# Gate chunks evicted by a plain copy, their sigmoid moved to the merge of the branches

## The chip, the cores and the metric

The kernel runs on one core of a Trainium2 chip. The metric is the device time of one execution in microseconds (us). The engines of the core are TensorE (PE for its matmuls, PEld for its weight loads), VectorE (DVE), ScalarE (ACT), GpSimd (POOL) and SyncE (SP); here POOL and SP mostly issue transfers. A matmul writes to PSUM, and another engine has to evict the result before the bank can be written again. Each engine takes its instructions in a fixed order. That order is settled when the program is built, by a scheduler that places one instruction after another.

## What is computed

One block of a hybrid network on 512 tokens of width 1024: a projection `u = h @ w_in`, two branches on it (RWKV time mixing and latent attention), a gated merge of the branches, an output projection, and then a large expert layer. What matters here is how the gates enter:

```python
u = h @ w_in[i]
gates = jax.nn.sigmoid(u[..., RW_COLS + MLA_COLS:]).reshape(B, T, N_BRANCHES, D)
...
merged = gates[:, :, 0] * (y_rw @ w_br_rwkv[i]) + gates[:, :, 1] * (y_mla @ w_br_mla[i])
x = x + merged @ w_out[i]
```

## The kernel before

Activations lie transposed, features on the partitions and 512 tokens along the free axis. The 4384 columns of `w_in` are taken in 35 chunks of 128, each a weight tile of 512 KB. Every product is formed in three parts from a high and a low half (`mm3`, L137): `hi*xh`, `hi*xl`, `lo*xh`. The high half of a weight is made by ACT (`whi`, L132), the low half by DVE (`wlo`, L133); L147 and L148 do the same for activations (`split`). A chunk with its 8 contraction steps is 24 matmuls.

The last 16 chunks are the gates, 8 for each branch. `gates` (L633) computes a chunk with `uchunk`, takes the sigmoid on ACT straight from PSUM into a tile `gt` (L637), and SP stores it to `gates_d` in DRAM (L638). Six gate chunks fill in beside the preparation of the time mixing (`prep`, PSUM tag `u` with one bank), four follow while DVE computes a triangular inverse (`inverse`, L555), and six stand before the recurrence (`chain`), beside the first steps of the attention (`attn`).

In `prep` ACT computes sigmoids (`sg` L416, `a` L420), exponentials (`E` L425) and square roots (L213), in the attention exponentials (`e` L879). Where the next function is not in the table that ACT holds, a table load stands in its order (ACT_TABLE_LOAD). A plain copy needs none in any of these places.

The merge comes after the branches. `wbr(1)` (L962) multiplies the attention's output with `w_br` in 8 units of 12 matmuls, one for each chunk of 128 outputs, and `wbr(0)` does the same for the time mixing. For every unit a gate chunk is fetched from `gates_d` by POOL's queue (L970) into a tile `gt` that has two buffers. In the first half the product `gt * ps` goes to `mp` (L980). In the second half `gt * ps` (L1002) and the sum with `mp` (L1003) are written in place, and `split` makes the halves `mh` and `ml` (L1004), so a buffer is free again only after `ml`. The 16 fetches are called the 1st to the 16th gate below, in the order of use. The PSUM tag `mm` has two banks, so a unit can start only when the product two units before it is done. Between the units ACT and DVE also convert weights: those of `w_br`, the input `pT` (`ph`, `pl`) and the two weights `w_pp`, whose raw tile is single-buffered. Then `w_out` follows in 8 chunks of 24 matmuls (L1006), which contract over all `mh` and `ml` and use the same two banks, and then the expert layer, by far the longest part.

Of the kernel before, what the change touches and what calls it, by code (L numbers as in the profile page):

```python
# [25 lines left out]
AF = mybir.ActivationFunctionType  # L26
# [86 lines left out]
def phase1(nc, tc, A, dbg):  # L113
# [10 lines left out]
    def wload(src, pl=None, row=False):  # L124
        own = pl is s.E or pl is s.PL
        raw = (pl if own else s.W).tile([128, 8, 128], F32, name="wraw", bufs={s.E: RAWB, s.PL: 1}[pl] if own else 3)
        nc.sync.dma_start(raw, src)
        s.nw += 1
        pl = pl or (s.WX if s.WX and s.nw % 3 == 0 else s.W)
        hi = pl.tile([128, 8, 128], F32R, name="whi", **(dict(tag="row", bufs=ROWS) if row else {}))  # L130
        lo = pl.tile([128, 8, 128], F32R, name="wlo", **(dict(tag="row", bufs=ROWS) if row else {}))
        nc.scalar.activation(hi, raw, AF.Copy)  # L132
        (nc.gpsimd if s.nw <= NWP else nc.vector).tensor_sub(lo, raw, hi.bitcast(F32))  # L133
        return hi, lo
    s.wload = wload

    def mm3(out, hi, lo, xh, xl, ks):  # L137

        n = len(ks)
        for i, (kw, kx) in enumerate(ks):  # L140
            nc.tensor.matmul(out, hi[:, kw], xh[:, kx], start=(i == 0), stop=False)  # L141
            nc.tensor.matmul(out, hi[:, kw], xl[:, kx], start=False, stop=False)  # L142
            nc.tensor.matmul(out, lo[:, kw], xh[:, kx], start=False, stop=(i == n - 1))  # L143
# [37 lines left out]
    def mm_tile(shape=(128, 512), tag="mm"):  # L181
        return (ppc if tag in "cu" else pp).tile(list(shape), F32, name=tag, tag=tag, bufs=1 if tag == "u" else None)
# [76 lines left out]
    def uchunk(oc, tag="mm", pl=None, raw=None):  # L259
        hi, lo = raw or wload(A["w_in"][oc], pl)  # L260
        ps = mm_tile(tag=tag)
        mm3(ps, hi, lo, *(XR if raw else (xh, xl)), [(k, k) for k in range(8)])
        return ps
# [369 lines left out]
    def gates(i0, i1, tag="u", pl=None):  # L633
        for i in range(i0, i1):
            ps = uchunk(19 + i, tag, pl)
            gt = MU.tile([128, T], F32, name="gt")
            nc.scalar.activation(gt, ps, AF.Sigmoid)  # L637
            nc.sync.dma_start(gates_d[i], gt)  # L638
            yield UNS

    oth = itertools.chain(others(), gates(0, NG))
    drive(prep(), oth)
    for _ in oth:
# [174 lines left out]
    def attn():  # L818
# [68 lines left out]
        def trans(n):  # L887
            e = EU[n]
            pt = mm_tile((128, 4, 128), tag="c" if n >= TC else "mm")
            for kb in range(4):  # L890
# [56 lines left out]
    for _ in gates(NG, NG + GK, GT):  # L947
        pass
# [3 lines left out]
    for _ in gates(NG + GK, 16, GT, GW):  # L952
        pass
# [8 lines left out]
    def wbr(b):  # L962
        for j in range(4):
            hi, lo = wload(A["w_br"][b * 4 + j])
            for o in range(2):
                oc = j * 2 + o
                ps = mm_tile(tag="mm")
                mm3(ps, hi, lo, yh, yl, [(o * 4 + k, k) for k in range(4)])
                gt = HM.tile([128, T], F32, name="gt")
                nc.gpsimd.dma_start(gt, gates_d[b * 8 + oc])  # L970
                yield oc, ps, gt

    HM = pool(name="hm", bufs=2, side="right")
# [5 lines left out]
    for oc, ps, gt in wbr(1):  # L979
        nc.vector.tensor_mul(mp[:, oc], gt, ps)  # L980
# [13 lines left out]
    for oc, ps, gt in wbr(0):  # L994
        if oc == 0:
            praw = PL.tile([128, 8, 128], F32, name="wraw", bufs=1)
            nc.sync.dma_start(praw, A["pT"].rearrange("p a (b t) -> p (a b) t", t=128))
            plh = PL.tile([128, 8, 128], F32R, name="ph", bufs=1)
            pll = PL.tile([128, 8, 128], F32R, name="pl", bufs=1)
            split(plh, pll, praw)  # L1000
            pw = [wload(A["w_pp"][k].rearrange("p (k c) -> p k c", k=8), PL) for k in range(2)]
        nc.vector.tensor_mul(gt, gt, ps)  # L1002
        nc.vector.tensor_add(gt, gt, mp[:, oc])  # L1003
        split(mh[:, oc], ml[:, oc], gt)  # L1004
    s.nsum = mm_tile((128, 4, 1), "s")
    for oc in range(8):  # L1006
        hi, lo = wload(A["w_out"][oc])
        ps = mm_tile()
# [8 lines left out]
    for tb in range(4):  # L1017
        for half in range(2):
            ps = mm_tile()
# [24 lines left out]
GT = "mm"  # L1044
EN = "a"
NWP = 0
TC = 99
LT_ = 2
LP = 3
# [498 lines left out]
```

## Time and profile before

| | us |
|---|---|
| median of three runs (1907.16 to 1909.44) | 1909.21 |
| the profiled execution, its own time | 1906.74 |
| its span, first to last instruction | 1904.8 |
| around the span (1906.74 - 1904.8) | 1.9 |
| PE busy | 1817.9 (95%) |
| DVE busy | 1540.0 (81%) |
| ACT busy | 830.6 (44%) |

The kernel falls into stretches: preparation with the first gates (to about 250 us), inverse with the other gates (250 to 323), recurrence and attention (to 484), merge (484 to 539), output projection and norm (to about 600), expert layer (to the end). A share of busy time is an average over all of them; what a change in one stretch is worth is read from the instructions there and from what each was waiting for.

### The profile page before, as it was taken

How to read it: one execution, taken by the hardware profiler on the slowest of the kernel's cores; microseconds unless marked ns; L12 is line 12 of the kernel's file. 1: busy time of each engine (PE TensorE's matmuls, PEld its weight loads, DVE VectorE, ACT ScalarE, POOL GpSimd, SP SyncE). 2: the span in 40 equal slices, each digit the busy share in tenths (PEclk: the TensorE clock that was granted, in tenths of full speed). 3: DMA queues.
4: the chain of work that ended last, by engine and by line, in shares of the span. 5: the costliest groups of instructions: out<-in, count | busy, mean ns of one | idle time of the engine just before them, and what ended most of it. 6: DMA issues, size and time to landing. Idle time of an engine off the chain costs nothing.

```text
span 1904.8 us, 29766 instructions
## 1 busy us (share of the span) xinstructions
PE 1817.9 (95%) x10969; PEld 1568.0 (82%) x10969; DVE 1540.0 (81%) x3103; ACT 830.6 (44%) x1227; POOL 464.4 (24%) x449
## 2 busy tenths in 40 slices
PE   8999868998999998999999999999999999999997
PEld 6777646776777888999999988888888888888775
DVE  7766778898855889999998956878787888777777
ACT  5656434665323334344444543333333333333354
POOL 1111321220101000332332021334344444344000
PEclk9999979998999999999999999999999999999999
DMA  4355655762434333789999799899999999999862
GB/s 170 117 154 150 184 161 167 224 200 83 149 105 143 101 101 94 240 307 360 359 340 345 281 348 350 312 346 343 326 335 333 344 351 347 327 334 338 291 215 99
DMA packets 196721, 470.19 MB, mean 247 GB/s; under 512 B 33312, under 2 KB 100896, under 8 KB 192736
## 3 DMA queue, kind: packets, MB, share of 16 engines
q1 hardware_dynamic: 146688, 273.23, 43.3%
q0 software_dynamic: 49744, 194.80, 29.1%
q8 instruction: 86, 1.41, 0.3%
q14 instruction: 59, 0.48, 0.1%
q10 hardware_dynamic: 144, 0.26, 0.0%
HBM read 397.97 MB, written 70.25 MB: 246 GB/s over the span
## 4 chain that ended last, share of the span: by engine, by line
PE 71%; DVE 12%; issue 7%; DMA 5%; ACT 3%; POOL 1%; SPq 0%; POOLq 0%; DVEq 0%; ACTq 0%
PE po L1498 26%; PE pa L1150 6%; PE pa L1148 6%; PE pa L1149 6%; PE mm L141 3%; PE mm L142 3%; PE mm L143 3%; PE po L1377 2%; DVE wlo L133 2%; PE q L141 2%; PE q L142 2%; PE q L143 2%; PE c L464 1%; DMA gt<-gates_d 1%; PE g L1178 1%
## 5 line engine op out<-in xcount | busy, mean ns | idle before, releaser
L132 ACT ACTIVATE whi<-wraw 128x1024 fp32r<-128x1024 f32 x352 | 370.6, 1059 | 457.5 <-PE pa L1149 156.0
L133 DVE TENSOR_TENSOR wlo<-wraw,whi 128x1024 fp32r<-128x1024 f32 x352 | 427.7, 1220 | 96.8 <-ACT whi L132 89.7
L1150 PE MATMUL pa<-hh,wlo 128*128 128x384 f32 x1024 | 347.8, 340 | 4.9 <-DVE wlo L133 4.8
L1148 PE MATMUL pa<-hh,whi 128*128 128x384 f32 x1024 | 348.8, 341 | 2.3 <-ACT ga L1156 1.3
L1149 PE MATMUL pa<-hl,whi 128*128 128x384 f32 x1024 | 347.5, 339 | 0.0
L1085 POOL DMA_INDIRECT row<-in_u,e x128 | 163.3, 1276 | 421.4 <-DVE row L1093 328.6
L1498 PE MATMUL po<-wlo,wh 128*128 128x512 f32 x768 | 237.2, 390 | 0.3 <-DVE wlo L133 0.3
L1085 POOL DMA_INDIRECT row<-in_v,e x128 | 176.4, 1378 | 249.4 <-DVE acc L1103 216.7
L1498 PE MATMUL po<-whi,wl 128*128 128x512 f32 x768 | 237.1, 389 | 0.0
L1498 PE MATMUL po<-whi,wh 128*128 128x512 f32 x768 | 210.4, 390 | 7.4 <-ACT whi L132 4.9
L1103 DVE SCALAR_TENSOR_TENSOR acc<-row,pre,acc 128x1024 f32<-128x1024 f32 x127 | 162.8, 1282 | 62.8 <-DMA row<-in_v,e 62.3
L1150 PEld LDWEIGHTS pa<-hh,wlo 128*128 128x128 f32 x1024 | 193.1, 189 | 7.8 <-DVE wlo L133 5.9
L1148 PEld LDWEIGHTS pa<-hh,whi 128*128 128x128 f32 x1024 | 193.2, 189 | 6.5 <-ACT ga L1156 1.7
L1149 PEld LDWEIGHTS pa<-hl,whi 128*128 128x128 f32 x1024 | 193.2, 189 | 3.6
L1498 PEld LDWEIGHTS po<-whi,wh 128*128 128x128 f32 x768 | 143.0, 188 | 33.6 <-ACT whi L132 6.2
L1498 PEld LDWEIGHTS po<-whi,wl 128*128 128x128 f32 x768 | 144.2, 188 | 30.5
L1093 DVE SCALAR_TENSOR_TENSOR row<-row,h2t 128x1024 f32<-128x1024 f32 x128 | 155.3, 1217 | 13.8 <-DMA row<-in_u,e 13.5
L1498 PEld LDWEIGHTS po<-wlo,wh 128*128 128x128 f32 x768 | 143.4, 188 | 27.5 <-DVE wlo L133 0.7
L147 ACT ACTIVATE wh<-gl 128x384 fp32r<-128x384 f32 x72 | 37.8, 526 | 204.9 <-PE po L1498 204.9
L141 PE MATMUL mm<-xh,whi 128*128 128x512 f32 x184 | 74.6, 406 | 4.4 <-ACT gt L637 3.3
L147 ACT ACTIVATE wh<-ga 128x384 fp32r<-128x384 f32 x48 | 25.1, 524 | 116.5 <-PE po L1498 74.2
L142 PE MATMUL mm<-xl,whi 128*128 128x512 f32 x184 | 74.1, 403 | 0.0
(465 smaller groups left out, 3160.6 us busy)
## 6 DMA issues: line engine op xcount, KB each, us to landing
wraw<-in_uT SPq DMA_DIRECT2D x128, 512.0 KB
wraw<-in_v SPq DMA_DIRECT2D x128, 512.0 KB
gd<-st POOLq DMA_DIRECT2D x12, 2048.0 KB, 10.3
g<-gd SPq DMA_DIRECT2D x32, 768.0 KB
wraw<-in_w_in SPq DMA_DIRECT2D x35, 512.0 KB
pk<-pk_d SPq DMA_DIRECT2D x16, 1024.0 KB
ga_d<-gs SPq DMA_DIRECT2D x72, 192.0 KB
gl<-ga_d SPq DMA_DIRECT2D x72, 192.0 KB
```

What stands on the lines that cost most here:

```text
L132: nc.scalar.activation(hi, raw, AF.Copy)
L133: (nc.gpsimd if s.nw <= NWP else nc.vector).tensor_sub(lo, raw, hi.bitcast(F32))
L141: nc.tensor.matmul(out, hi[:, kw], xh[:, kx], start=(i == 0), stop=False)
L142: nc.tensor.matmul(out, hi[:, kw], xl[:, kx], start=False, stop=False)
L143: nc.tensor.matmul(out, lo[:, kw], xh[:, kx], start=False, stop=(i == n - 1))
L1085: nc.gpsimd.indirect_dma_start(out=r, out_offset=None, in_=table, in_offset=bass.IndirectOffsetOnAxis(ap=e3[:, hk:hk + 1], axis=0))
L1093: nc.vector.scalar_tensor_tensor(r, r, 1.0, h2t, op0=OP.mult, op1=OP.mult, accum_out=pre[:, u:u + 1])
L1103: nc.vector.scalar_tensor_tensor(acc, r, pre[:, u:u + 1], acc, op0=OP.mult, op1=OP.add)
L1148: nc.tensor.matmul(pa, hi[:, k], hh[:, k, 0:NDT], start=(k == 0), stop=False)
L1149: nc.tensor.matmul(pa, hi[:, k], hl[:, k, 0:NDT], start=False, stop=False)
L1150: nc.tensor.matmul(pa, lo[:, k], hh[:, k, 0:NDT], start=False, stop=(k == 7))
L1498: nc.tensor.matmul(po[tb][:, half], w[:, ts], v[:, hs], start=(m == 0 and w is wh and v is vh), stop=(m == 127 and w is wl))
```

## The change

The sigmoid in `gates` becomes a plain copy, put in a block of higher priority for the scheduler, with an offset of 1000 places. `gates_d` then holds values before the sigmoid. In `wbr` the sigmoid is taken in place on the fetched tile. Everything else is as it was.

```diff
@@ -634,7 +634,9 @@
         for i in range(i0, i1):
             ps = uchunk(19 + i, tag, pl)
             gt = MU.tile([128, T], F32, name="gt")
-            nc.scalar.activation(gt, ps, AF.Sigmoid)
+
+            with tc.high_priority(offset=EP):
+                nc.scalar.activation(gt, ps, AF.Copy)
             nc.sync.dma_start(gates_d[i], gt)
             yield UNS
 
@@ -968,6 +970,7 @@
                 mm3(ps, hi, lo, yh, yl, [(o * 4 + k, k) for k in range(4)])
                 gt = HM.tile([128, T], F32, name="gt")
                 nc.gpsimd.dma_start(gt, gates_d[b * 8 + oc])
+                nc.scalar.activation(gt, gt, AF.Sigmoid)
                 yield oc, ps, gt
 
     HM = pool(name="hm", bufs=2, side="right")
@@ -1044,6 +1047,7 @@
 GT = "mm"
 EN = "a"
 NWP = 0
+EP = 1000
 TC = 99
```

Line numbers of the changed kernel are two to four higher behind the first edit: its copy is L639, its fetch L972, its sigmoid L973, the products L983 and L1005, the sum L1006.

How the order of instructions moves is shown at three places, from the two built programs.

**ACT, beside the preparation**, at the first gate chunk (`whi` is a weight's high half, `sg` and `a` are the preparation's sigmoids, `E` its exponential). Before:

```order
L132 ACTIVATE whi<-wraw 128x1024
L637 ACT_TABLE_LOAD
L637 ACTIVATE gt<-u 128x512
L416 ACTIVATE sg<-c,vec 128x512
L420 ACTIVATE a<-c,vec 128x512
L440 ACTIVATE a<-a,oka,vec 128x512
L132 ACTIVATE whi<-wraw 128x1024
L425 ACT_TABLE_LOAD
```

Now:

```order
L132 ACTIVATE whi<-wraw 128x1024
L639 ACTIVATE gt<-u 128x512
L416 ACT_TABLE_LOAD
L416 ACTIVATE sg<-c,vec 128x512
L420 ACTIVATE a<-c,vec 128x512
L440 ACTIVATE a<-a,oka,vec 128x512
L132 ACTIVATE whi<-wraw 128x1024
L425 ACT_TABLE_LOAD
```

The copy stands where the sigmoid stood, and the load goes to the next sigmoid of the preparation. Over all 16 chunks the eviction keeps its place among its neighbours; the table loads at L637 (six) and at L879 (two) are gone, and four new ones stand at L416. Up to the merge PE, DVE, POOL and SP keep their order.

**ACT and DVE, in the merge**, from the conversion of `pT` on. ACT before (`mh` is the high half of the merged product):

```order
L147 ACTIVATE ph<-wraw 128x1024
L132 ACTIVATE whi<-wraw 128x1024 x4
L147 ACTIVATE mh<-gt 128x512
L132 ACTIVATE whi<-wraw 128x1024
L147 ACTIVATE mh<-gt 128x512
```

ACT now (the four sigmoids before these rows are those of the 1st to 4th gate; the first of them has a table load):

```order
L147 ACTIVATE ph<-wraw 128x1024
L973 ACTIVATE gt<-gt 128x512 x2
L132 ACTIVATE whi<-wraw 128x1024 x2
L973 ACTIVATE gt<-gt 128x512 x2
L132 ACTIVATE whi<-wraw 128x1024 x2
L973 ACTIVATE gt<-gt 128x512 x2
L132 ACTIVATE whi<-wraw 128x1024
L147 ACTIVATE mh<-gt 128x512 x2
L132 ACTIVATE whi<-wraw 128x1024
L973 ACTIVATE gt<-gt 128x512 x2
L147 ACTIVATE mh<-gt 128x512 x2
```

DVE before, from the first product of the second half on:

```order
L1002 TENSOR_TENSOR gt<-gt,mm 128x512
L1003 TENSOR_TENSOR gt<-gt,mp 128x512
L133 TENSOR_TENSOR wlo<-wraw,whi 128x1024
L148 TENSOR_TENSOR ml<-gt,mh 128x512
L1002 TENSOR_TENSOR gt<-gt,mm 128x512
L133 TENSOR_TENSOR wlo<-wraw,whi 128x1024
L1003 TENSOR_TENSOR gt<-gt,mp 128x512
L1002 TENSOR_TENSOR gt<-gt,mm 128x512
L148 TENSOR_TENSOR ml<-gt,mh 128x512
```

DVE now:

```order
L133 TENSOR_TENSOR wlo<-wraw,whi 128x1024 x2
L1005 TENSOR_TENSOR gt<-gt,mm 128x512
L1006 TENSOR_TENSOR gt<-gt,mp 128x512
L1005 TENSOR_TENSOR gt<-gt,mm 128x512
L133 TENSOR_TENSOR wlo<-wraw,whi 128x1024
L1006 TENSOR_TENSOR gt<-gt,mp 128x512
L148 TENSOR_TENSOR ml<-gt,mh 128x512 x2
L133 TENSOR_TENSOR wlo<-wraw,whi 128x1024
L1005 TENSOR_TENSOR gt<-gt,mm 128x512 x2
L1006 TENSOR_TENSOR gt<-gt,mp 128x512 x2
L148 TENSOR_TENSOR ml<-gt,mh 128x512 x2
```

The gates are now handled in pairs: both sigmoids, both products, both sums, both high and both low halves. The sigmoids of the 9th and 10th gate stand behind the second `whi` of the pair before them, which is that of the second `w_pp` weight.

**PE, behind the merge**, in the first two chunks of `w_out` (numbers tell the two PSUM tiles apart: `mm_5274` and `mm_5308` before, `mm_5290` and `mm_5324` now). Before, the last rows of both:

```order
L141 MATMUL mm_5308<-mh_5071,whi_5304 128x512
L141 MATMUL mm_5274<-mh_5071,whi_5270 128x512
L142 MATMUL mm_5308<-ml_5072,whi_5304 128x512
L143 MATMUL mm_5308<-mh_5071,wlo_5305 128x512
L141 MATMUL mm_5308<-mh_5071,whi_5304 128x512
L142 MATMUL mm_5274<-ml_5072,whi_5270 128x512
L143 MATMUL mm_5274<-mh_5071,wlo_5271 128x512
L142 MATMUL mm_5308<-ml_5072,whi_5304 128x512
L143 MATMUL mm_5308<-mh_5071,wlo_5305 128x512
```

Now, around the last rows of the first:

```order
L142 MATMUL mm_5290<-ml_5080,whi_5286 128x512
L143 MATMUL mm_5290<-mh_5079,wlo_5287 128x512
L141 MATMUL mm_5290<-mh_5079,whi_5286 128x512
L142 MATMUL mm_5290<-ml_5080,whi_5286 128x512
L143 MATMUL mm_5290<-mh_5079,wlo_5287 128x512
L143 MATMUL mm_5324<-mh_5079,wlo_5321 128x512
L141 MATMUL mm_5324<-mh_5079,whi_5320 128x512
L142 MATMUL mm_5324<-ml_5080,whi_5320 128x512
```

Before, the first chunk ends two matmuls ahead of the second; now it ends 19 matmuls ahead of it (its 24th matmul is the 29th of the 48).

## Rows read from the trace of the kernel before

**Rows 1.** the page: busy time, share of the span, instructions by engine

```profile
PE 1817.9 (95%) x10969; PEld 1568.0 (82%) x10969; DVE 1540.0 (81%) x3103; ACT 830.6 (44%) x1227; POOL 464.4 (24%) x449
```

**Rows 2.** stretches: busy us of each engine, then TensorE's granted clock, DMA share, GB/s

```profile
60.00:250.00 190.00, 179.99 (x924) 137.91 (x922) 132.61 (x208) 106.35 (x139) 49.45 (x68) 0.98 0.58 161
250.00:330.00 80.00, 62.45 (x235) 47.37 (x235) 64.92 (x167) 30.02 (x44) 11.95 (x17) 0.87 0.45 145
...
484.00:512.00 28.00, 27.38 (x118) 21.16 (x119) 22.69 (x47) 10.35 (x14) 4.31 (x9) 1.00 0.57 177
512.00:539.12 27.12, 23.18 (x89) 17.10 (x88) 18.56 (x26) 8.70 (x11) 3.76 (x7) 0.94 0.51 159
539.12:552.00 12.88, 12.16 (x51) 9.29 (x51) 6.28 (x9) 3.48 (x6) 0.00 (x0) 1.00 0.17 56
552.00:640.00 88.00, 84.57 (x392) 68.49 (x393) 56.12 (x183) 32.33 (x48) 8.77 (x12) 1.00 0.37 120
```

**Rows 3.** waits of PE, 60 to 250 us: total, times, longest; the longest one

```profile
PE c L488 <- DVE bk L480: 3.8, 1, 3.8
```

**Rows 4.** timeline of ACT, front part: start us, us, line, tiles, [idle before]

```profile
74.10 1.28 ACT L637 ACT_TABLE_LOAD   x1
75.40 0.60 ACT L637 ACTIVATE gt<-u 128x512 f32<-128x512 f32 x1
79.18 0.69 ACT L416 ACTIVATE sg<-c,vec 128x512 f32<-128x512 f32 x1 [3.19 <-PE c L414]
...
250.86 1.28 ACT L637 ACT_TABLE_LOAD   x1
...
325.66 1.28 ACT L879 ACT_TABLE_LOAD   x1
```

**Rows 5.** timeline of PE, then DVE, front part

```profile
252.80 0.79 PE L141 MATMUL mm<-xh,whi 128*128 128x512 f32 x1 [3.32 <-ACT gt L637]
272.74 0.80 PE L831 MATMUL mm<-wlo,cqh 128*128 128x512 f32 x1 [5.79 <-DVE wlo L133]
...
257.05 0.91 DVE L567 TENSOR_TENSOR xtmp<-U,X 128x31 f32<-128x31 f32 x2 [6.83 <-DMA U<-pk_d]
...
330.02 0.21 DVE L880 RECIPROCAL mx<-mx 128x1 f32<-128x1 f32 x2
```

**Rows 6.** timeline of ACT in the merge

```profile
515.42 1.06 ACT L132 ACTIVATE whi<-wraw 128x1024 fp32r<-128x1024 f32 x1 [3.99 <-DMA wraw<-in_w_pp]
```

**Rows 7.** timeline of POOL in the merge; then all gate DMAs' time to landing

```profile
518.64 0.54 POOL L970 DMA_DIRECT2D gt<-gates_d  x1 [5.47 <-DVE ml L148]
523.02 0.54 POOL L970 DMA_DIRECT2D gt<-gates_d  x1 [3.83 <-DVE ml L148]
537.55 0.54 POOL L970 DMA_DIRECT2D gt<-gates_d  x1 [2.17 <-DMA wraw<-in_w_out]
...
DMA to landing us min/median/max: 2.7/3.0/4.8
```

**Rows 8.** timeline of DVE in the merge

```profile
513.39 0.68 DVE L1002 TENSOR_TENSOR gt<-gt,mm 128x512 f32<-128x512 f32 x1
538.29 0.69 DVE L1002 TENSOR_TENSOR gt<-gt,mm 128x512 f32<-128x512 f32 x1 [1.03 <-PE mm L143]
```

**Rows 9.** timeline of PE in the merge and after it

```profile
527.17 0.50 PE L141 MATMUL mm<-yh,whi 128*128 128x512 f32 x1 [1.87 <-DVE gt L1002]
539.12 0.47 PE L141 MATMUL mm<-mh,whi 128*128 128x512 f32 x1 [0.86 <-DVE gt L1002]
550.96 0.50 PE L141 MATMUL mm<-mh,whi 128*128 128x512 f32 x1 [0.50 <-ACT whi L132]
551.90 0.50 PE L141 MATMUL mm<-mh,whi 128*128 128x512 f32 x1 [0.22 <-ACT whi L132]
```

**Rows 10.** groups by line, ACT: busy us, mean ns, idle before

```profile
L1027 ACT ACTIVATE pst<-mm 128x512 f32<-128x512 f32 x8 | 4.8, 600 | 8.7 <-DMA pp_d<-pst 7.7 <-PE mm L1025 0.7 <-PE pa L227 0.3
L538 ACT ACTIVATE lg<-lg 128x512 f32<-128x512 f32 x1 | 0.6, 632 | 0.9 <-DVE lg L369 0.9
```

## The prediction, made before the result was known

> **What bounds the kernel now.** Read the page's busy times first: TensorE is busy 95% of the span, ACT 44% [rows 1]. Less work on ACT is therefore worth nothing by itself; only what TensorE waits for counts. The table of stretches says where TensorE has room: from 60 to 250 us it is busy 179.99 of 190 us at clock 0.98, from 250 to 330 only 62.45 of 80 at 0.87, in the first half of the merge 27.38 of 28, in its second half 23.18 of 27.12 at 0.94, and behind it in the expert layer 84.57 of 88 [rows 2]. Two consequences. A delay at the end of the merge is not made good later, as the expert layer has 3.4 us of slack in 88 and that slack sits in its own dependences: I carry a delay over one to one. And the change can matter in three places only: the front, where table loads go; the second half of the merge, where sigmoids come; and the start of `w_out`.
>
> Then the waits of TensorE in the first gates' stretch: the longest is 3.8 us, for DVE (`bk`, L480) [rows 3]; none of its long waits is for the gate eviction. The single one anywhere that is, stands at 252.80 [rows 5].
>
> **The front: copies for sigmoids.** The eviction itself keeps its price. The sigmoid out of PSUM takes 0.60 us [rows 4], a plain copy of the same shape out of PSUM 0.600 [rows 10]. It keeps its place too: in the built order copy and sigmoid have the same neighbours, so the "at once" of the edit, its priority block, moves nothing. What goes is table loads, 1.28 us each [rows 4]: six at L637 and two at L879 go, four come at L416, so ACT saves 4 x 1.28 = 5.1 us by these counts. Where do they lie?
>
> - In the preparation the load moves from ahead of the eviction to ahead of `sg`. There ACT had waited 3.19 us for TensorE's `c` [rows 4], so the new load lies in that wait. TensorE is nearly full in this stretch and waits for DVE: gain 0. ACT's 106.35 of 190 us [rows 2] says the same.
> - At 250.86 the load goes with nothing in its place. The eviction ends 1.28 us sooner, and TensorE, which had waited 3.32 us for it, starts at 251.5 instead of 252.80. What is late next? DVE's inverse starts at 257.05, after 6.83 us of waiting for a transfer (`U` from `pk_d`), and TensorE later stands 5.79 us at 272.74 for a `wlo` that DVE makes between inverse steps [rows 5]. The 1.28 us fill that wait. Gain 0, at best 1.3 if the `wlo` moves too.
> - The load at 325.66 [rows 4] stands ahead of an attention exponential; the pass behind it needs a DVE row that is made at 330.02 [rows 5]. Gain 0.
>
> So the front gives 0 (0 to -1.3).
>
> The Trainium skill, "ScalarE: Activation LUTs", section "Table sets: the hidden batching unit", says to batch activations by set; this change does so, and speaks for a gain. Its section "What ACT_TABLE_LOAD costs" adds a drain of about 1.38 us to a load of 1.283 us. By that page four loads would be an estimated 10.6 us of ACT's time. The trace agrees on the load (1.28) and shows no drain: the activation at 75.40 begins 0.02 us after the load's end [rows 4].
>
> **The merge's first half.** Eight sigmoids and one load are added. TensorE is full here (27.38 of 28) [rows 2], and a fetched gate waits for its product; a sigmoid of 0.63 us, the price of one from SBUF to SBUF [rows 10], fits between. Cost 0 (0 to 0.6).
>
> **The merge's second half** is where the added sigmoids reach the path. SP's and POOL's queues keep their order, but what POOL's fetches wait for becomes later. Step by step:
>
> 1. The sigmoids of the 9th and 10th gate stand, on ACT, behind the `whi` of the second `w_pp` weight, which waits 3.99 us for its transfer and runs 515.42 to 516.48 [rows 6]. So the 9th product, at 513.39 before [rows 8], starts at 516.48 + 0.6 = 517.05: 3.7 us later.
> 2. `mh` and `ml` of the 9th now stand behind the 10th's product and sum. From the 9th product to the fetch of the 11th: four passes of 0.69 [rows 8] and one weight conversion (1.06 on ACT [rows 6], not less on DVE) with the handovers, 4.1 to 5.2 us; before it was 518.64 - 513.39 = 5.25 [rows 7, 8]. I take 4.85: fetch of the 11th at 521.9, 3.3 late. The 12th follows one pass later, about 522.5, against 523.02: 0.5 us early. The even gates keep their times, the odd ones lose.
> 3. From then on a pair is a loop, since two buffers hold two gates: landing 3.0 [rows 7], sigmoid 0.63 [rows 10], products of both, sum, high and low half at 0.69 each [rows 8] = 3.4, together 7.1. With handovers, and a `w_out` conversion in one of them, 7.3 to 8.3; I take 7.9. The 15th gate is fetched at 521.9 + 2 x 7.9 = 537.7, and its product starts at 537.7 + 3.0 + 0.63 = 541.3, against 538.29 [rows 8]: +3.0.
> 4. `w_out` needs the bank that this product frees. Before it started 0.83 us after the product's start, at 539.12 [rows 8, 9]; now at 542.1. **+3.0** (+1.8 by 7.3, +3.8 by 8.3).
>
> **Behind it.** In `w_out` the first chunk's last matmul is now the 29th of 48 instead of the 46th. The conversions of the third weight are thus covered, where TensorE had waited 0.50 and 0.22 us [rows 9]: -0.7, up to -1.4 if the wait's second half goes too. I take **-1.0**.
>
> **The clock.** With the same TensorE work until then, TensorE stands about 3 us more in this half, mostly in one wait just ahead of `w_out`. Such waits have been followed by the lower clock here: the half with the wait of 1.87 us at 527.17 has a mean granted clock of 0.94, or (1 - 0.94) x 27.12 = 1.6 us lost; 250 to 330 has 0.87, 10.4 us lost over some four long waits, 2.6 each. After a wait of 0.86 us the clock stayed at 1.00 [rows 2, 9]. An added wait of 3 us lies nearer to the former: **+2.1** (0 to +2.6).
>
> **Sum:** 0 + 0 + 3.0 - 1.0 + 2.1 = +4.1 us. Against the profiled execution's own 1906.74 us that is 1910.8; the median of before is 2.5 us above it, and by the median the forecast is 1909.21 + 4.1 = **1913.3 us**. A measurement of this kernel tells about 0.2%, 3.8 us, from no change, so the forecast lies just above that line.
>
> **The rivals.**
>
> - *Faster: the front is paced by ACT.* If the loads lay on the path in spite of ACT's 44%, the net four would give 4 x 1.28 = 5.1 us: 1904.1 us. For it speaks TensorE's wait of 3.32 us at 252.80, which the load made longer [rows 5]; against it the 3.8 us wait for DVE and the 3.19 us of ACT waiting for TensorE [rows 3, 4]. It decides if the merge costs under 1.3 us. Chance 0.10. By the Trainium skill's batching rule and its 2.66 us for a switch ("ScalarE: Activation LUTs", "What ACT_TABLE_LOAD costs") the time would be an estimated 1898.6; the missing drain speaks against it.
> - *Within 0.2%: no clock loss.* The merge goes as above, but TensorE's added wait is cut into two or three short ones, since the even gates keep their schedule. Then the 2.1 us fall away: +2.0, 1911.2 us. For it speaks the clock of 1.00 after 0.86 us [rows 2, 9]. Chance 0.32.
> - *Slower still: paired fetches collide.* Two fetches now go out 0.6 us apart, each of 256 KB, together with weights. Landing is 3.0 us in the median and 4.8 at most [rows 7]. With 4.8 in the three pairs, +5.4: 1918.7 us. Against it: the fetches of before stood beside the same weight traffic and had 3.0. Chance 0.10.
> - *The change doesn't do what it says.* That the copy is not "at once" is settled by the built order, and is in the forecast; this has no chance of its own.
>
> **How the numbers follow.** Forecast 0.48, of which 0.08 falls below the 0.2% line as its terms vary; no clock loss 0.32; faster 0.10; colliding fetches 0.10. Faster by over 0.2% 0.10; within 0.32 + 0.08 = 0.40; slower 0.40 + 0.10 = 0.50. Range: the low end has -1.3 in the front, +1.8, -1.4 and no clock loss, -0.9, so 1908.3; the high end +3.8 - 0.7 + 2.6 and one landing of 4.8 instead of 3.0, +7.5, so 1916.7. Rounded outward, 1908 to 1917; the first and the third rival stay outside, 2 in 10.
>
> **What would show it.** In the timeline of ACT the loads ahead of gate evictions are gone, those at L416 end before the `c` they wait for, and the merge begins within 1.3 us of its old time; a start 3 us or more earlier proves the front wrong. In the merge, the 9th sigmoid starts right after a `whi`, the 11th gate is fetched near 521.9 and the 12th near 522.5, the 15th product starts near 541.3; if the 11th is fetched before 520, steps 1 and 2 are wrong. `w_out` starts 3 us later relative to the merge's start, its waits for `whi` are gone, and the clock of the stretch around its start is below 1.00; if it is 1.00, the second rival holds.

## The result, and the profile after

The change makes the kernel slower. Its median is 1919.13 us (9 executions, 1911.62 to 1926.0) against 1908.75 for the kernel before; the ratio is 1.0054 with a 95% interval of 1.0036 to 1.0071, that is +10.3 us (+6.9 to +13.6). The forecast was +4.1 us and 1913.3 us, with a range from 1908 to 1917. The sign was right, the size was not.

The profiled execution has a span of 1919.3 us. The page's busy times, to be held against [rows 1], show no new bound:

```profile
PE 1824.2 (95%) x10969; PEld 1573.3 (82%) x10969; DVE 1543.2 (80%) x3103; ACT 834.9 (43%) x1240; POOL 461.4 (24%) x449
```

The stretches, as in [rows 2] (busy us of PE, PEld, DVE, ACT, POOL, then the granted clock, DMA share, GB/s), show where it went. Up to 512 us TensorE does what it did before; the second half of the merge is 31.70 us long instead of 27.12; and the first chunks of `w_out`, at clock 1.00 before, run at 0.87, which costs (1 - 0.87) x 12.88 = 1.7 us.

```profile
60.00:250.00 190.00, 179.97 (x924) 137.82 (x923) 132.46 (x208) 105.70 (x138) 49.48 (x68) 0.98 0.59 161
250.00:330.00 80.00, 61.51 (x235) 46.45 (x235) 65.03 (x167) 24.66 (x40) 11.92 (x17) 0.87 0.44 146
484.00:512.00 28.00, 26.50 (x112) 19.88 (x112) 23.04 (x48) 16.21 (x23) 4.16 (x8) 1.00 0.52 171
512.00:543.70 31.70, 24.22 (x95) 18.30 (x94) 19.39 (x26) 13.74 (x19) 3.89 (x8) 0.95 0.48 151
543.70:556.58 12.88, 12.88 (x49) 10.37 (x50) 4.96 (x7) 2.81 (x4) 0.00 (x0) 0.87 0.18 59
```

**The front.** In ACT's timeline (start, us, engine, line, tiles; in brackets the idle time before and what ended it) the copy takes 0.58 us where the sigmoid took 0.60 [rows 4], and the load moved to L416 lies in the wait for TensorE's `c`. TensorE starts 1.05 us earlier at the next chunk, and has 0.21 us of that left 21 us later, where it waits 6.18 us for DVE's `wlo` instead of 5.79 [rows 5].

```profile
74.13 0.58 ACT L639 ACTIVATE gt<-u 128x512 f32<-128x512 f32 x1
74.73 1.28 ACT L416 ACT_TABLE_LOAD   x1
79.33 0.69 ACT L416 ACTIVATE sg<-c,vec 128x512 f32<-128x512 f32 x1 [3.31 <-PE c L414]
...
251.75 0.79 PE L141 MATMUL mm<-xh,whi 128*128 128x512 f32 x1 [1.91 <-ACT gt L639]
...
272.53 0.79 PE L833 MATMUL mm<-wlo,cqh 128*128 128x512 f32 x1 [6.18 <-DVE wlo L133]
```

**The merge.** First ACT: the 9th sigmoid stands behind the `whi` of the second `w_pp` weight; from the 11th on they come in pairs, each behind a landing.

```profile
514.40 1.06 ACT L132 ACTIVATE whi<-wraw 128x1024 fp32r<-128x1024 f32 x1 [2.97 <-DMA wraw<-in_w_pp]
515.44 0.64 ACT L973 ACTIVATE gt<-gt 128x512 f32<-128x512 f32 x1
...
525.65 1.27 ACT L973 ACTIVATE gt<-gt 128x512 f32<-128x512 f32 x2 [1.51 <-DMA gt<-gates_d]
...
532.92 1.27 ACT L973 ACTIVATE gt<-gt 128x512 f32<-128x512 f32 x2 [3.41 <-DMA gt<-gates_d]
...
542.30 1.24 ACT L973 ACTIVATE gt<-gt 128x512 f32<-128x512 f32 x2 [1.24 <-DMA gt<-gates_d]
```

Then POOL's fetches (the 11th to 16th gate, to be held against [rows 7]), and DVE's products of the 9th and of the 15th and 16th gate (against [rows 8]):

```profile
521.82 0.54 POOL L972 DMA_DIRECT2D gt<-gates_d  x1 [9.09 <-DVE ml L148]
522.61 0.54 POOL L972 DMA_DIRECT2D gt<-gates_d  x1 [0.25 <-DVE ml L148]
529.93 1.14 POOL L972 DMA_DIRECT2D gt<-gates_d  x2 [6.78 <-DVE ml L148]
538.36 1.14 POOL L972 DMA_DIRECT2D gt<-gates_d  x2 [7.29 <-DVE ml L148]
...
516.63 0.68 DVE L1005 TENSOR_TENSOR gt<-gt,mm 128x512 f32<-128x512 f32 x1
...
542.96 1.29 DVE L1005 TENSOR_TENSOR gt<-gt,mm 128x512 f32<-128x512 f32 x2 [0.65 <-ACT gt L973]
```

TensorE waits for it in two long pieces, where [rows 9] had 1.87 and 0.86; the waits of 0.50 and 0.22 us for `whi` behind the start of `w_out` are gone:

```profile
527.05 0.50 PE L141 MATMUL mm<-yh,whi 128*128 128x512 f32 x1 [3.82 <-DVE gt L1005]
543.70 0.50 PE L141 MATMUL mm<-mh,whi 128*128 128x512 f32 x1 [3.51 <-DVE gt L1005]
```

`w_out` starts at 543.70 instead of 539.12: +4.6 us. Until the end of the span the distance grows to 14.5 us (1919.3 - 1904.8).

### The profile page after: what moved, and what is told of

Read it like the earlier page. It is cut to its first block, busy times and chain, and to the rows that moved or that the text cites. A ratio compares the mean times of both kernels' runs of the same rounds, so it can differ in the third digit from the quotient of the medians.

```text
span 1919.3 us, 29785 instructions
## 1 busy us (share of the span) xinstructions
PE 1824.2 (95%) x10969; PEld 1573.3 (82%) x10969; DVE 1543.2 (80%) x3103; ACT 834.9 (43%) x1240; POOL 461.4 (24%) x449
## 3 DMA queue, kind: packets, MB, share of 16 engines
q0 software_dynamic: 49744, 194.80, 28.9%
## 4 chain that ended last, share of the span: by engine, by line
PE 69%; DVE 11%; issue 8%; DMA 6%; ACT 4%; POOL 1%; SPq 0%; DVEq 0%; POOLq 0%; ACTq 0%
PE po L1502 26%; PE pa L1152 6%; PE pa L1154 6%; PE pa L1153 6%; PE mm L141 3%; PE mm L142 3%; PE mm L143 3%; PE po L1381 2%; PE q L141 2%; PE q L142 2%; PE q L143 2%; DVE wlo L133 1%; DMA wraw<-in_uT 1%; PE c L464 1%; DMA row<-in_u,e 1%
## 5 line engine op out<-in xcount | busy, mean ns | idle before, releaser
L1089 POOL DMA_INDIRECT row<-in_v,e x128 | 170.3, 1331 | 257.0 <-DVE acc L1107 233.3
L1152 PEld LDWEIGHTS pa<-hh,whi 128*128 128x128 f32 x1024 | 193.7, 189 | 10.5 <-ACT gs L1160 4.0
L143 PE MATMUL mm<-xh,wlo 128*128 128x512 f32 x184 | 73.5, 399 | 0.0
```

The source lines that it names most:

```text
L1089: nc.gpsimd.indirect_dma_start(out=r, out_offset=None, in_=table, in_offset=bass.IndirectOffsetOnAxis(ap=e3[:, hk:hk + 1], axis=0))
L1152: nc.tensor.matmul(pa, hi[:, k], hh[:, k, 0:NDT], start=(k == 0), stop=False)
```

## The experiments

Sixteen kernels ran in five sets; each set was timed beside runs of the kernel before on its own chip. Three questions were asked: front or merge; what in the merge; and why the full time loses 10 us when the merge's trace shows 5.

### Front or merge

**Front alone.** The sigmoid at the merge is left out, so no gate gets one.

```diff
-                nc.scalar.activation(gt, gt, AF.Sigmoid)
```

> Leaves the sigmoid of the gates out altogether (plain copy at the eviction, nothing at the merge), so all engines but ACT keep the order of before. Theory 1 (the whole loss comes from the merge on): 0, between -1.5 and +1.5 us; in the profile the wait of TensorE at 252.8 us is about 1 us shorter and nothing of that is left at 275 us. Rival (the front's moved table loads disturb something that shows late): +3 to +6 us of the +10.

Measured: ratio 1.0015 (1.0001 to 1.0028), +2.9 us (+0.2 to +5.3), above the 1.5 that was expected at most. An unchanged kernel gave +1.3 (-1.1 to +4.0, see the control), so a small loss here can't be told from nothing, and most of the +10 isn't here. A gain from four fewer table loads isn't here either.

**Merge alone.** The kernel before, with a plain in-place copy where the changed kernel has its sigmoid.

```diff
                 nc.gpsimd.dma_start(gt, gates_d[b * 8 + oc])
+                nc.scalar.activation(gt, gt, AF.Copy)
```

> The kernel before, with a plain in-place copy of each fetched gate by ACT at the place where the changed kernel has its sigmoid; sigmoids and table loads of the front stay. Theory 1: the merge alone makes the loss, so the time is that of the changed kernel, +10 us (+7 to +13), and w_out starts 4 to 5 us late. Rival (front): +4 to +6 us only.

Measured: 1.0044 (1.0027 to 1.0062), +8.4 us (+5.2 to +11.8); `w_out` starts 5.0 us late. The sigmoid as such and its table load don't matter: a copy in its place does nearly the same.

**The priority offset.**

```diff
-EP = 1000
+EP = 0
```

> The changed kernel with the priority offset 0 instead of 1000; every engine's order is the same as with 1000. It is a second look at the changed kernel on another occasion: +10 us (+7 to +13) if the priority offset does nothing. Theory 1a (a delayed expert layer reliably loses more): in its profile the shift of TensorE against before is 5 to 6 us at 800 us and 9 us or more at 1000 us. Theory 1b (the loss behind 800 us in the one profile was chance): 5 to 6 us at 800 us and the same, within 2, at the end, while the median still lies above +7.

Measured: 1.0055 (1.0036 to 1.0075), +10.5 us. All engines keep their order, so the offset is void, and the loss came again. In its profile TensorE is 6.6 us late at the start of `w_out`, 8.4 at 815 us and 14.0 at the end: the loss behind `w_out` came again too. Most of it stands in one place in both profiles: between the matmuls at 785 and 852 us of before this kernel loses 6.0 us and the changed kernel 5.2.

### What in the merge

**Fewer sigmoids, one by one.** Only the second half's gates (9th to 16th) take their sigmoid at the merge.

```diff
-                nc.scalar.activation(gt, ps, AF.Copy)
+                nc.scalar.activation(gt, ps, AF.Copy if i < 8 else AF.Sigmoid)
...
-                nc.scalar.activation(gt, gt, AF.Sigmoid)
+                if b == 0: nc.scalar.activation(gt, gt, AF.Sigmoid)
```

> Only the 9th to 16th gate are evicted plainly and take their sigmoid at the merge; the scheduler then keeps the gates one by one, with DVE in the order of before, instead of in pairs. Theory 2 (the pairs make most of the delay: both fetches wait for the low halves of both): w_out starts 1 to 3 us late, the fetch of the 11th at 518.6 to 520, and the time is +1 to +5 us. Rival (any added pass of ACT between landing and product makes it, in pairs or not): w_out 4 us or more late, the time +8 to +11 us.

Measured: 1.0025 (1.0010 to 1.0039), +4.8 us (+1.9 to +7.4), but the merge in its profile is 54.70 us long against 54.62: eight sigmoids in the critical half, at no cost there. The scheduler had not paired the gates. `w_out` was expected 1 to 3 us late and started 1.0 early; what the +4.8 is made of isn't shown, as fifteen sigmoids, below, cost 0.6.

**Fifteen sigmoids, single or in pairs.** These two kernels differ in nothing but the gate that keeps its sigmoid at the eviction, the 5th (`i == 12`) or the 6th (`i == 13`) in the order of use. With the first the scheduler handles the second half gate by gate; with the second, in pairs as in the changed kernel.

```diff
-                nc.scalar.activation(gt, ps, AF.Copy)
+                nc.scalar.activation(gt, ps, AF.Sigmoid if i in (12,) else AF.Copy)
...
-                nc.scalar.activation(gt, gt, AF.Sigmoid)
+                if b * 8 + oc not in (12,): nc.scalar.activation(gt, gt, AF.Sigmoid)
```

> The changed kernel, but the 5th gate in the order of use keeps its sigmoid at the eviction; the other 15 take it at the merge. With this the scheduler keeps the second half one gate at a time (sigmoid, high half, sigmoid, high half). Theory 2 (the pairs make the merge's delay): the merge, from its first matmul to the start of w_out, is within 1.5 us of the 54.6 us of before; the time +1 to +4 us, no more than the unchanged kernel and the front-only kernel showed. Rival (the number of passes that ACT gets between landing and product makes it): merge +4 to +6 us, time +7 to +11.

> The same with the 6th gate in place of the 5th: 15 sigmoids at the merge as well, but the scheduler handles the second half in pairs, as in the changed kernel. Theory 2: merge +4 to +6.5 us, time +7 to +11. Rival: the same as the kernel with the 5th gate left out, whatever that gives.

Measured: single 1.0003 (0.9992 to 1.0015), pairs 1.0050 (1.0030 to 1.0070). The same fifteen passes cost nothing one by one and 9.6 us in pairs. ACT's timeline of the single kernel shows the difference: the 9th sigmoid runs ahead of the `w_pp` conversion, not behind it, and the 10th comes after that:

```profile
511.06 0.63 ACT L973 ACTIVATE gt<-gt 128x512 f32<-128x512 f32 x1 [1.67 <-DMA gt<-gates_d]
513.23 1.06 ACT L132 ACTIVATE whi<-wraw 128x1024 fp32r<-128x1024 f32 x1 [1.54 <-DMA wraw<-in_w_pp]
514.69 0.63 ACT L973 ACTIVATE gt<-gt 128x512 f32<-128x512 f32 x1 [0.40 <-DMA gt<-gates_d]
```

TensorE's waits in the single kernel, then in the pair kernel (whose merge begins 5.6 us later in its profile):

```profile
521.49 0.50 PE L141 MATMUL mm<-yh,whi 128*128 128x512 f32 x1 [2.22 <-DVE gt L1005]
...
537.24 0.50 PE L141 MATMUL mm<-mh,whi 128*128 128x512 f32 x1 [1.92 <-DVE gt L1005]
```

```profile
531.52 0.79 PE L141 MATMUL mm<-yh,whi 128*128 128x512 f32 x1 [4.82 <-DVE gt L1005]
...
547.82 0.50 PE L141 MATMUL mm<-mh,whi 128*128 128x512 f32 x1 [3.31 <-DVE gt L1005]
```

Read from the timelines of nine kernels (merge: TensorE's first matmul of L962 to the start of `w_out`; all in us):

| kernel | merge start to 9th product | 9th to 15th product | merge |
|---|---|---|---|
| before | 28.9 | 24.9 | 54.6 |
| before, control | 29.9 | 23.8 | 54.5 |
| front alone | 29.1 | 25.8 | 55.8 |
| second half, single | 30.0 | 24.0 | 54.7 |
| fifteen, single | 29.6 | 24.8 | 55.1 |
| changed | 32.2 | 26.3 | 59.2 |
| changed, offset 0 | 32.7 | 27.4 | 60.9 |
| fifteen, pairs | 32.3 | 27.0 | 60.1 |
| copies at the merge | 32.9 | 27.0 | 60.6 |

The last four are the paired ones. They lose in two places: about 3 us up to the 9th product, and 2 to 3 in the loop behind it. Both come with the same order of instructions, so no run shows what each is worth by itself.

**Buffer free early.** A buffer's release set the pace already before; here the sum goes to `mp`, so that the gate's buffer is free before the two halves are made.

```diff
-        nc.vector.tensor_add(gt, gt, mp[:, oc])
-        split(mh[:, oc], ml[:, oc], gt)
+        nc.vector.tensor_add(mp[:, oc], gt, mp[:, oc])
+        split(mh[:, oc], ml[:, oc], mp[:, oc])
```

> The kernel before, with the sum written to mp instead of in place, so that a gate's buffer is free after the sum and not after the low half; no sigmoid is moved. Theory 2 (two buffers and what holds them set the pace of the second half already before): w_out starts 1 to 3 us early, the wait of 1.87 us at 527.2 is gone or below 1, the time -1 to -5 us. Rival (TensorE's own work and the weights set the pace there): w_out within 0.5 us of before, the time within 1.5 us.

Measured: 0.9996 (0.9979 to 1.0013), the merge 53.7 us. The theory's numbers were missed, and the time is the rival's: the wait at the place of the 1.87 us is 2.10. In POOL's timeline the fetches go out in pairs here too (519.85 and 521.18, 527.81 and 529.13), and the next product waits 2.81 us for its landing. The same edit on the kernel with fifteen single sigmoids:

> The single-gate kernel with the sum written to mp, so that a buffer is free before the two halves are made. Theory 2: the merge is at or below that of before, -2 to +0.5 us, and the time 0 to +3 us; whether it beats the kernel before is not expected, since the front gave nothing. Rival (the sigmoids cost in the loop after all): merge +2 or more.

Measured: **0.9963 (0.9950 to 0.9976), -7.1 us**: faster than both kernels. The merge is 51.0 us long, there is one wait over 0.5 us left in it, and its second half runs at clock 1.00 (0.94 before, [rows 2]):

```profile
526.58 0.50 PE L141 MATMUL mm<-yh,whi 128*128 128x512 f32 x1 [0.60 <-DVE gt L1005]
...
508.83:531.95 23.12, 22.52 (x95) 17.43 (x95) 19.49 (x26) 13.26 (x20) 4.30 (x8) 1.00 0.63 195
```

I had expected no gain here. With only the second half's eight sigmoids moved:

> Only the 9th to 16th gate take their sigmoid at the merge, one by one, and the sum goes to mp, so that a buffer is free before the halves are made; the front keeps eight of its sigmoids. It tells where the gain of the faster kernel (15 single sigmoids, early free) comes from. Theory 3 (from the merge: no wait over 1 us and no fall of the clock there): merge -2.5 to -4 us against the 54.6 of before, time -3 to -7 us. Rival (from the front, where that kernel has seven more plain copies): merge as in the early-free kernel alone, -1, and the time within 2 us of before.

Measured: 0.9983 (0.9967 to 0.9998), -3.2 us (-6.3 to -0.4); the merge is 52.8 us long, 1.8 less than before, where theory 3 had 2.5 to 4, and one wait of 1.19 us is left in it. The kernel keeps eight sigmoids in the front and still has a shorter merge, so a gain can be had from the merge without the front; that seven more copies in the front add something isn't ruled out, as its gain is half the other's. What these two kernels win is won in the loop: from the 9th to the 15th product they take 20.1 and 19.0 us, where all others of the table take 23.8 or more. Up to the 9th product they take 31.9 and 31.2, nearly as long as the paired ones.

### Why 10 us and not 5

**A plain delay.** The kernel before, with nine (or four) in-place copies of the 15th gate ahead of its product.

```diff
+        for _ in range(9 if oc == 6 else 0): nc.scalar.activation(gt, gt, AF.Copy)
         nc.vector.tensor_mul(gt, gt, ps)
```

> The kernel before, with nine more in-place copies by ACT of the 15th gate ahead of its product, some 5 us, so that TensorE waits some 4 to 5 us longer at the start of w_out and nothing else changes up to there; the order behind w_out is the same. Theory 1a: a delay of the expert layer costs more than itself, +8 to +11 us. Theory 1b / rival (delay carried one to one): the wait plus one fall of the clock less the covered conversions, +4 to +6 us.

> The kernel before, with four more in-place copies of the 15th gate ahead of its product: w_out starts some 2 us late. Theory 1b (one to one, plus at most one fall of the clock): +1.5 to +4 us. Theory 1c (each wait behind a delay can gain or lose a fall of the clock, whatever the delay's size): anything from 0 to +8, not in proportion to the 5 us kernel.

Measured: nine copies 1.0021 (1.0010 to 1.0031), +4.0 us, with the merge 4.7 longer in the profile; four copies 1.0016 (1.0002 to 1.0029), +3.1 us, with the merge 3.8 longer. Within these intervals (+1.9 to +5.9 and +0.4 to +5.5 us) a delay ahead of `w_out` is carried one to one. The delays were not in proportion to the copies; they are read from the profile. With nine copies the wait at the start of `w_out` is at least that of the changed kernel (3.51):

```profile
544.27 0.47 PE L141 MATMUL mm<-mh,whi 128*128 128x512 f32 x1 [4.05 <-DVE gt L1003]
```

**Control.** The kernel before, unchanged.

> The kernel before, unchanged, as a second look at its own expert layer. Theory 1c: its time is within 0.1% of before, but its profile differs from the first by several us behind 700 us, with the clock falling at other waits. Rival (the expert layer of before is always as in the first profile, and only a changed front or merge disturbs it): TensorE's times agree within 1 us to the end.

Measured: 1.0007 (0.9994 to 1.0021). Two executions of one program differ behind `w_out`: the control's start of `w_out` is 2.1 us early, and its end 1.6 us late. It waits here, where the first profile of before has no wait over 0.5 us (the changed kernel waits 3.27 us at this matmul, where ACT comes late with `gs` after 5.49 us of waiting for a weight). The control's row, then those of the changed kernel:

```profile
824.63 0.45 PE L1148 MATMUL pa<-hh,whi 128*128 128x384 f32 x1 [2.25 <-ACT gs L1156]
...
829.52 1.06 ACT L132 ACTIVATE whi<-wraw 128x1024 fp32r<-128x1024 f32 x1 [5.49 <-DMA wraw<-in_uT]
832.43 0.69 PE L1152 MATMUL pa<-hh,whi 128*128 128x384 f32 x1 [3.27 <-ACT gs L1160]
```

**Cut kernels.** Everything behind the output projection is left out (the norm and the expert layer), and `x1T` is written out. The order up to there is that of the full kernels.

```diff
-        phase2(nc, tc, s, A, out, None)
+        phase2_(nc, tc, s, A, out, None)
```

> The kernel before, cut off behind the output projection: the norm and the whole expert layer are left out, and the projection's result is written out as it is. The order of every engine up to the end of the output projection is that of the full kernel. It is the base for the three other cut kernels; by the full kernel's trace (585 us to the end of the projection) it takes 595 to 620 us.

> The changed kernel, cut off in the same way. Theory A (the changed kernel's front and merge themselves cost more over many executions than the profiles of the paired kernels showed, 4.8 to 6.3 us): +8 to +11 us against the cut kernel before. Theory B (they cost what the profiles show, and the rest of the +10 is lost in the expert layer): +4.5 to +6.5 us.

> The kernel with nine added copies of the 15th gate, cut off in the same way. Both theories: +4 to +6 us, as its profile shows (4.7 + 0.2) and its full time (+4). If the full kernel's +4 hides a larger delay, it is +7 or more here.

> The faster kernel (15 single sigmoids, buffer free early), cut off in the same way. If its -7 us is made in front and merge: -6 to -8 us. If the merge gives what its profile shows (-3.7) and the rest is gained in the expert layer: -3 to -4.5 us.

Measured, as means of 5 or 6 executions each (their standard deviation is 1.3 to 1.9 us, so a difference has a standard error of about 1 and is good to some 2): before 614.0; changed 619.5, **+5.5** (+3.5 by the medians); nine copies 619.5, +5.6; fifteen single and free early 610.8, -3.2. Theory B fits and theory A doesn't: up to the projection the change costs about what the profiles show (4.6 + 0.2). That leaves 10.3 - 5.5 = 4.8 us of the changed kernel's loss, with an uncertainty of some 4, in the expert layer, and about as much of the faster kernel's gain (-7.1 + 3.2 = -3.9); for the plain delay nothing is left (4.0 - 5.6 = -1.6).

**The clock over all executions.** The granted clock was read in each execution. (1 - clock) x span, the time that the lower clock takes if TensorE is busy, is 38.8 us in the mean of the changed kernel's nine executions, against 33.0 to 34.5 in the five sets of the kernel before. In the other paired kernels it is 39.2 (copies at the merge), 38.1 (offset 0) and 40.5 (fifteen in pairs); with fifteen single it is 34.9. So about 5 of the 10 us go with a lower clock, good to some 2. In the cut kernels the same difference is 2.9 (31.6 against 28.7). Some 2.4 us are left for the expert layer, half of the 4.8, with an uncertainty as large.

**What stays open** is why the paired order costs more there. In the profiles the stretch from the last matmul of `w_out` to the end of the span does not sort the kernels: paired ones 1323.3 to 1329.8 us, the others 1320.1 (the first profile of before, the shortest of all) to 1332.6. Counted by TensorE's matmuls, most of the 9.7 us between the profiles of before and of the changed kernel stands in two places: 5.2 us between the matmuls at 785 and 852 us of before, around the wait for `gs` shown above, and 2.9 behind the one at 1672. But the control loses 3.5 us at the first place, and the kernel of before with its buffer free early, which is no slower, 6.3. One profile of each kernel thus shows where time can go there, and not which kernel loses it.

## Why the prediction was wrong, step by step

**Front: 0 (0 to -1.3).** Right. The merge of the changed kernel begins at 484.48 us, before at 484.50. That these two agree so well is chance, as the start lies between 481.3 and 487.8 in the eighteen profiles; but the eight with the front of before have 483.7 in the mean, and the four with copies for all sixteen gates 483.4. The gain at 252.80 [rows 5] was 1.05 us, and the wait for `wlo` took it, as forecast. The rival of a front paced by ACT is out. The Trainium skill ("ScalarE: Activation LUTs", section "Table sets: the hidden batching unit") asks for batches by table set; the change does that, and the trace shows ACT's time saved (130.4 us busy from 60 to 330 us instead of 136.4) at no gain: behind the one long wait that a load had lengthened stood another, for DVE.

**First half: 0 (0 to 0.6).** Nearly right: TensorE is busy 26.50 of 28 us instead of 27.38, or 0.9 less, where 0.6 was the bound.

**Second half, steps 1 and 2.** Right to half a microsecond: the 9th product was forecast at 517.05 and stands at 516.63, the fetch of the 11th at 521.9 and 521.82, of the 12th at 522.5 and 522.61. Part of this is luck: the conversion ahead of the 9th sigmoid began 1.0 us earlier than before (514.40), the product came 1.2 us behind its end instead of 0.6, and from the product to the 11th's fetch it took 5.2 us instead of 4.85.

**Step 3, the first that failed.** The term was +3.0 and measured +4.6: the 15th product was forecast at 541.3 and stands at 542.96. From the 11th's fetch on I had two loops of 7.9 and a landing of 3.0 with a sigmoid. The loops took 8.1 and 8.4 (521.82, 529.93, 538.36). The landing was mis-sized: from fetch to sigmoid 3.83, 2.99 and 3.94 us, 10.8 in sum instead of 9.0. I took the median of the gates of before, 3.0 [rows 7]; in the changed kernel the median of all is 3.3 and the longest 5.2, and why is not shown. That is not the rival of colliding fetches: the single kernel fetches one at a time and its odd gates took as long (3.0, 3.6 and 3.9). That this rival's time, 1918.7, lies near the measured one is chance.

**The reason given.** I put the delay down to sigmoids added on the path, with pairs as the form they take. The runs show that the form is all of it: fifteen passes one by one cost 0.6 us (-1.5 to +2.9).

**Behind it: -1.0, and the clock: +2.1.** Near: together +1.1 was forecast, and the stretch from the first to the last matmul of `w_out` is 0.2 us longer; with 1.7 us lost to the clock, the covered conversions gave 1.5. But I had counted the merge's waits as one of 3 us; there were two, of 3.82 and 3.51. So by the profile the change costs 4.6 + 0.2 = 4.8 us up to the end of `w_out`, and by the cut kernels 5.5: near the +4.1 that was forecast for the whole. The miss is mostly behind it.

**"I carry a delay over one to one", the second that failed.** The stretch that I read it from, 552 to 640 us, is output projection and norm up to about 600; it holds 40 us of an expert layer of 1300. The plain delays bear the step out; the paired kernels don't, by some 5 us (10.3 - 5.5 = 4.8, good to some 4). The clock term belongs to this: it had one fall, +2.1, and over all executions the clock takes about 5 us more, about half of it behind the projection. What brings the rest, and why the clock is lower there, stays open. I had also measured against a profiled execution that was a good one: its stretch behind `w_out` is the shortest of all fourteen full kernels profiled. So the distance of 14.5 us between the two profiled executions is not all the change's.

**Range and chances.** The bounds had one landing of 4.8 instead of 3.0 and one fall of the clock; neither had anything for the expert layer, which takes two thirds of the time. The rival within 0.2% is out, as the clock did fall.

## What to carry to other kernels

Read an added pass by the order that the scheduler makes of it, not by its length: what cost here was an order in which two gates shared two buffers in lockstep and the first stood behind a conversion that waits for a transfer. Where a loop is paced by few buffers, look for the last reader of each: taking the two halves off the gate's buffer gave 0.4% together with a single order, and nothing that can be measured without it. And before a difference of 0.2% is worked out from one profiled execution, find out how long the parts behind the change take in a second one.

## What the runs showed of the hardware

The same wait may or may not be followed by the lower clock. Behind the output projection, TensorE waits for the eviction `pst`: before, 2.49 us; in the changed kernel, 2.31. In the expert layer it waits 2.96 and 2.98 us at one and the same matmul. The rows of before, waits and then the stretch around each:

```profile
594.03 0.50 PE L1023 MATMUL mm<-whi,ph 128*128 128x512 f32 x1 [2.49 <-ACT pst L1027]
...
1775.01 1.66 PE L1498 MATMUL po<-whi,wh 128*128 128x512 f32 x6 [2.96 <-ACT whi L132]
...
593.00:600.00 7.00, 5.97 (x28) 4.85 (x29) 2.45 (x4) 3.69 (x7) 2.16 (x4) 1.00 0.37 140
1774.00:1780.00 6.00, 4.99 (x22) 4.13 (x23) 3.20 (x4) 2.54 (x3) 0.00 (x0) 1.00 1.03 403
```

And those of the changed kernel:

```profile
598.64 0.50 PE L1026 MATMUL mm<-whi,ph 128*128 128x512 f32 x1 [2.31 <-ACT pst L1030]
...
1786.61 2.33 PE L1502 MATMUL po<-whi,wh 128*128 128x512 f32 x6 [2.98 <-ACT whi L132]
...
598.00:606.00 8.00, 7.36 (x28) 5.91 (x29) 2.24 (x4) 3.85 (x7) 2.16 (x4) 0.79 0.35 131
1786.00:1792.00 6.00, 5.39 (x17) 4.28 (x18) 3.43 (x4) 1.61 (x2) 0.00 (x0) 0.72 1.02 399
```

The clock stays at 1.00 in the first kernel and falls in the second, where (1 - 0.79) x 8 and (1 - 0.72) x 6 are 1.7 us each; at its lowest, from 600 to 602 and from 1788 to 1790 us, the granted clock is 0.50, half of full. The length of a wait alone thus does not decide it, as my clock term had assumed. The Trainium skill ("TensorE: Matmul & The Clock Gate", section "What's actually happening") says that what the gate looks at is "free-running" and doesn't restart with the kernel; these rows agree with that and don't prove it. Three such falls, 5.1 us, would be the part of the loss that goes with a lower clock; what sets them off isn't shown.
